# Unit 0's seven low parts move to VectorE, and pair 1's four GpSimd subtractions are issued behind pair 2's norm

## The chip, the cores and the metric

One core of a Trainium2 chip runs the kernel. The metric is the device time of one execution in microseconds (us); the time of a kernel is the median of its runs. TensorE (PE in the profile) multiplies, VectorE (DVE), ScalarE (ACT) and GpSimd (POOL) work elementwise, and SyncE's queue (SP) starts the transfers.

## What is computed

The reference is one layer of an encoder on two sequences of 512 tokens with 16 shared meta tokens in front: a convolution branch and an attention branch beside each other, then a gated feed-forward network (FFN), then a norm. The change lies where the first part ends and the FFN begins:

```python
h = h + jnp.concatenate([u, o], axis=-1) @ w_out[i]
hf = _rms(h, ffn_norm_g[i])
h = h + (jax.nn.silu(hf @ w_gate[i]) * (hf @ w_up[i])) @ w_down[i]
```

`h` is 1024 tokens by 1024, `w_gate` and `w_up` are 1024 by 2816.

## The kernel before

**High and low parts.** Every operand of a product is split in two: the high part is the float32 number cast to TensorE's fp32r format (on ACT), the low part is what the cast left over (number minus high part, one subtraction). `mm3` makes a product out of three matmuls, high by high, high by low and low by high.

**Tokens.** The 1024 tokens are eight tiles of 128, kept in `hres[0]` to `hres[7]` (in the profile `h` or `slots`). Tile t of the first sequence and tile t + 4 of the second are called pair t here. A `w_out_block` (dq, t), block (dq, t) in the text, multiplies 128 tokens by 256 columns of `w_out` and adds the result to `hres[t]` on DVE (L994). This addition is what empties PE's bank, and the text calls it the drain of the block. In the prediction, block (2,7) is columns 512 to 767 of tile 7. The banks come from `bank()`, a ring of four, which the FFN's products use as well: a block or product can begin when the drain of the fourth one before it is through.

**The norm of a pair.** `sq(t)` stores the finished `hres[t]` in DRAM, squares and sums it on ACT (L192), and on POOL adds epsilon (L193) and takes the power -1/2 (L194, the tile `rs`). `sc(t)` multiplies the tile by `rs` and the gain on DVE, in two halves (L1045, the tiles `hf` and `tt`).

**The turn of a pair.** The FFN multiplies 2 by 2 blocks in the manner of Strassen and Winograd, with seven products in place of eight, so it needs sums of the four quarters of a pair's activations. `tu(t, s)` transposes a tile on PE (L1060). `do(t, stages)` then forms the operands: stages a and A copy and cast on ACT; b takes two low parts on DVE; c, e and d form the sums on DVE (L1086, L1087, L1091, L1094) and cast them on ACT; x takes the low parts of s2 and s3, y those of s1 and s4 (all L1067). Which engine does x and y is set by the table `S_DVE`: GpSimd for pairs 0 to 2, DVE for pair 3.

**The weights.** A unit is 128 columns of `w_gate` (even units) or `w_up` (odd ones); there are 22. `comb(j)`, in the schedule `co(j)`, prepares the j-th of a unit's seven weight operands: for some j it first subtracts blocks on DVE (L1136: t1 and t2 at j = 2, t3 at 3, t4 at 5), then ACT casts the high part (L1152), then the low part is subtracted (L1154), on GpSimd unless the unit's number is in the table `U0_DVE`. `product(j)`, in the schedule `pr(j)`, is the product itself; its results are taken from the bank at L1165 to L1188.

**The order.** In this part of the kernel every instruction of PE, DVE, ACT and GpSimd is pinned, so each engine works in the order in which the program issues them. That order is a list written by hand, in which a tuple is a block and the rest are the steps named above; the seven `co` stand among the last blocks, and the list is followed by unit 0's first half-products, the turn of pair 3 (whose norm is `sc(3)` and `sc(7)`) and the other half-products. `units[1].load` loads the weights of unit 1 into `hres[2]` and `hres[6]`, once pair 2's low parts no longer need them. Each engine works through its own list, waiting where an instruction needs another engine's result.

Of the kernel before, what the change touches and what calls it, by code (L numbers as in the profile page):

```python
# [83 lines left out]
QL_DVE = False  # L84
LO_W = 1024
ORDER = "Q K S0 S1 T0 T3 M0 T1 M1 S2 T2 M2 T4 M4 M3 S3 E C"
U0_DVE = ()
S_DVE = ((), (), (), (0, 1, 2, 3))


# [11 lines left out]
def encoder_kernel(ctx: ExitStack, tc: tile.TileContext, x, meta, gains, w_in, w_kr, small, conv_w, wq, wk, wv,  # L102
# [22 lines left out]
    def pin(ins):  # L125

        return in_order(ins) if pinned[0] else ins
# [914 lines left out]
    def ffn_scale(t):  # L1042
        for e in range(2):
            h, g = (a[:, e * 512:(e + 1) * 512].rearrange("p (k n) -> p k n", k=4) for a in (hres[t], g_ffn))
            pin(nc.vector.scalar_tensor_tensor(normed_half(t, e), h, ffn_rs[t], g, ALU.mult, ALU.mult))  # L1045

    class Turn:
# [21 lines left out]
        def do(self, stages):  # L1069
            b11, b12 = self.pts[0]  # L1070
            b21, b22 = self.pts[1] if len(self.pts) > 1 else (None, None)
            t1, t2, t3, t4 = self.ts
            own = [nc.vector if i in S_DVE[self.t] else nc.gpsimd for i in range(4)]
            for stage in stages:
                if stage == "a":
                    self.high(a11, b11)
                    pin(nc.scalar.copy(t1, b11))
                    self.high(a12, b12)
                elif stage == "A":
                    pin(nc.scalar.copy(t4, b22))  # L1080
                    self.high(a22, b22)
                elif stage == "b":
                    self.low(a11, b11, nc.vector)
                    self.low(a12, b12, nc.vector)
                elif stage == "c":
                    pin(nc.vector.tensor_sub(t3, t1, b21))  # L1086
                    pin(nc.vector.tensor_sub(t1, b22, t3))  # L1087
                    self.high(s2, t1)
                    self.high(s3, t3)
                elif stage == "e":  # L1090
                    pin(nc.vector.tensor_sub(t2, b12, t1))  # L1091
                    self.high(s4, t2)
                elif stage == "d":
                    pin(nc.vector.tensor_add(t4, t4, b21))  # L1094
                    self.low(a22, b22, nc.vector)
                    self.high(s1, t4)
                elif stage == "x":
                    self.low(s2, t1, own[0])
                    self.low(s3, t3, own[1])
                elif stage == "y":  # L1100
                    self.low(s1, t4, own[2])
                    self.low(s4, t2, own[3])
# [15 lines left out]
    class Unit:  # L1118
# [19 lines left out]
        def comb(self, j):  # L1138
# [13 lines left out]
            pin(nc.scalar.copy(w[:, 0:512], src))  # L1152
            lo_eng = nc.vector if self.u in U0_DVE else nc.gpsimd
            pin(lo_eng.tensor_sub(w[:, 512:1024], src, w[:, 0:512].bitcast(F32)))  # L1154
# [96 lines left out]
    def sq(t):  # L1251
        return lambda: ffn_square(t)

    def sc(t):
        return lambda: ffn_scale(t)

    def co(j):
        return lambda: units[0].comb(j)
# [6 lines left out]
    def tu(t, s):  # L1265
        def begin():
            if not s:
                turns[t] = Turn(t)
            turns[t].turn(s)
        return begin  # L1270

    def do(t, stages):
# [5 lines left out]
         (1, 5), do(0, "ce"), (2, 5), do(0, "d"), (3, 5), sq(5), do(0, "x"),  # L1278
         (0, 2), sc(1), (1, 2), sc(5), do(0, "y"), (2, 2), (3, 2), sq(2), tu(1, 0), do(1, "a"), (0, 6), tu(1, 1), do(1, "A"),
         do(1, "b"), (1, 6), do(1, "ce"), (2, 6), do(1, "d"), (3, 6), sq(6),  # L1280
         (0, 3), sc(2), do(1, "x"), (0, 7), sc(6), co(0), do(1, "y"), (1, 3), tu(2, 0), do(2, "a"), co(1), (1, 7),
         tu(2, 1), do(2, "A"), do(2, "b"), co(2), (2, 3), co(3), do(2, "ce"), (2, 7), do(2, "d"), co(4), (3, 3), sq(3),
         co(5), (3, 7), sq(7), co(6)])

# [9 lines left out]
    def reuse(key):  # L1294
        pool = ops if key.startswith("act") else comb
        return pool.tile([P, 4, SEQ], F32R, tag=key, bufs=1, name=name("re")).rearrange("p a b -> p (a b)")
# [141 lines left out]
    y, junk = (reuse(ld_places[i]).bitcast(F32) for i in (0, 1))  # L1438
# [93 lines left out]
```

## Time and profile before

| | us |
|---|---|
| median of 3 runs | 1099.79 (1099.77 to 1099.86) |
| the profiled execution, its own time | 1100.08 |
| its span, first to last instruction | 1098.3 |
| PE busy | 1075.8 |
| DVE busy | 829.0 |
| ACT busy | 497.5 |
| POOL busy | 475.9 |

A row of the order in time gives the start in us, the time in us (of all instructions that the row merges), the engine, the line, the operation, output and inputs by the program's names, their shapes, and how many instructions the row holds; a bracket gives the idle time of the engine before it and the event that ended it. Times are counted from the span's start. An instruction's time overlaps a little with the next one's start: two drains in a row take 0.74 us, each alone 0.41. The part that the change touches lies between 440 and 482 us; the granted clock of TensorE is 1.00 there.

### The profile page before, as it was taken

To read this page: it belongs to the slowest core of one execution; us is meant where nothing else is said; L and a number is where in the kernel's file an instruction comes from. 1 tells how busy PE (TensorE), PEld (TensorE's weight loads), DVE (VectorE), ACT (ScalarE), POOL (GpSimd) and SP (SyncE) were. 2 spreads that over 40 slices of the span, in tenths; PEclk is the share of its full clock that TensorE was granted. 3 is DMA by queue.
4 is the path that set the end of the run, shared out by engine and by line. 5 is a ranking of instruction groups with operands and counts; after the bars stand their busy time and mean duration, and the time that the engine had idled before them with its cause. 6 is when DMAs were issued, how large, how long until landed. Compare 5 with 4: busy or idle time off the path is not lost.

```text
span 1098.3 us, 16027 instructions
## 1 busy us (share of the span) xinstructions
PE 1075.8 (98%) x5922; PEld 929.5 (85%) x5922; DVE 829.0 (75%) x1206; ACT 497.5 (45%) x836; POOL 475.9 (43%) x419
## 2 busy tenths in 40 slices
PE   8999999999999999899999999999999999999997
PEld 8989888888888999788888888888888888888886
DVE  5699997888887646999877876877687496656643
ACT  6554525787786534542223233322322355433331
POOL 4689735564563233775544554554555200000012
PEclk9999999999999999999999999999999999999999
DMA  7211111110100412245445426444543899865503
GB/s 295 78 39 44 44 39 61 39 55 4 40 22 35 157 58 97 77 148 186 130 160 192 169 94 207 164 140 148 201 157 103 298 329 338 293 197 182 182 22 133
DMA packets 71422, 147.08 MB, mean 134 GB/s; under 512 B 6944, under 2 KB 29728, under 8 KB 71344
## 3 DMA queue, kind: packets, MB, share of 16 engines
q1 hardware_dynamic: 71344, 146.06, 38.9%
q8 instruction: 47, 0.77, 0.3%
q14 instruction: 31, 0.25, 0.1%
HBM read 105.92 MB, written 40.11 MB: 133 GB/s over the span
## 4 chain that ended last, share of the span: by engine, by line
PE 56%; DVE 2%; issue 2%; DMA 0%; POOL 0%; ACT 0%; POOLq 0%; ACTq 0%; SPq 0%; DVEq 0%
PE pt L167 48%; PE ps L167 8%; DMA raw<-in_w_gate_dram 0%; DVE tt L1045 0%; DVE hf L1045 0%; DVE tt L1136 0%; DVE slots L994 0%; DVE act_l L1067 0%; POOL rs L194 0%; DVE h L1087 0%; POOL slots L1442 0%; DVE slots L1086 0%; DVE slots L1094 0%; DVE a12l L1067 0%; DVE h L1091 0%
## 5 line engine op out<-in xcount | busy, mean ns | idle before, releaser
L167 PE MATMUL pt<-act_h,wc 128*128 128x512 f32 (+1 forms) x552 | 175.1, 380 | 0.0
L1154 POOL TENSOR_TENSOR wc<-tt,wc 128x512 fp32r<-128x512 f32 x88 | 124.6, 1432 | 104.4 <-ACT wc L1152 60.2
L167 PEld LDWEIGHTS pt<-act_h,wc 128*128 128x128 f32 x552 | 102.5, 188 | 19.6
L193 POOL TENSOR_SCALAR ms<-ms 128x1 f32<-128x1 f32 x15 | 7.3, 485 | 242.6 <-ACT re L192 214.1
L167 PE MATMUL pt<-hn_h,wp 128*128 128x512 f32 (+2 forms) x448 | 107.0, 331 | 0.0
L167 PE MATMUL pt<-act_l,wc 128*128 128x512 f32 (+1 forms) x276 | 104.8, 380 | 0.0
L1152 ACT CAST wc<-tt 128x512 fp32r<-128x512 f32 x88 | 51.4, 617 | 116.5 <-PE pt L167 109.8
L1334 DVE TENSOR_TENSOR re<-re,re 128x1024 fp32r<-128x1024 f32 x53 | 64.1, 1223 | 45.9 <-ACT re L1333 45.8
L1333 ACT CAST re<-re 128x1024 fp32r<-128x1024 f32 x53 | 55.0, 1054 | 69.2 <-PE ps L167 20.0
L167 PE MATMUL pt<-re 128*128 128x512 f32 x360 | 84.0, 389 | 0.0
L167 PEld LDWEIGHTS pt<-hn_h,wp 128*128 128x128 f32 x448 | 75.8, 188 | 8.5
L167 PEld LDWEIGHTS pt<-re 128*128 128x128 f32 x360 | 67.6, 188 | 14.0
L152 POOL TENSOR_TENSOR wp<-raw,wp 128x1024 fp32r<-128x1024 f32 x24 | 58.5, 2439 | 40.5 <-ACT wp L149 40.5
L167 PE MATMUL pt<-hn_l,wp 128*128 128x512 f32 (+2 forms) x224 | 74.5, 332 | 0.0
L742 POOL TENSOR_SCALAR p<-p,sst 128x512 f32<-128x512 f32 x64 | 44.1, 696 | 65.3 <-DVE sst L740 57.4
L167 PE MATMUL pt<-wp,act_h 128*128 128x256 f32 x384 | 71.2, 285 | 0.0
L1154 POOL TENSOR_TENSOR wc<-raw,wc 128x512 fp32r<-128x512 f32 x33 | 45.5, 1390 | 52.1 <-ACT wc L1152 52.1
L167 PE MATMUL ps<-re 128*128 128x512 f32 x276 | 63.9, 389 | 0.0
L367 POOL TENSOR_TENSOR pacc<-pacc,prod 128x512 f32<-128x512 f32 x43 | 58.3, 1355 | 7.0 <-ACT prod L365 4.3
L167 PEld LDWEIGHTS ps<-re 128*128 128x128 f32 x276 | 51.8, 188 | 10.7
L167 PEld LDWEIGHTS pt<-act_l,wc 128*128 128x128 f32 x276 | 51.9, 188 | 9.8
L167 PEld LDWEIGHTS pt<-wp,act_h 128*128 128x128 f32 x384 | 59.9, 192 | 0.2
(296 smaller groups left out, 2937.5 us busy)
## 6 DMA issues: line engine op xcount, KB each, us to landing
raw<-in_w_gate_dram SPq DMA_DIRECT2D x22, 512.0 KB, 3.9
hf<-in_w_down_dram SPq DMA_DIRECT2D x44, 256.0 KB, 4.8
re<-in_w_down_dram SPq DMA_DIRECT2D x31, 256.0 KB, 5.3
raw<-in_w_in_dram SPq DMA_DIRECT2D x12, 512.0 KB, 3.6
slots<-in_w_up_dram SPq DMA_DIRECT2D x11, 512.0 KB, 3.5
h<-in_w_up_dram SPq DMA_DIRECT2D x11, 512.0 KB, 5.5
d_t1t<-hf SPq DMA_DIRECT2D x22, 256.0 KB, 5.4
d_t4t<-hf SPq DMA_DIRECT2D x22, 256.0 KB, 2.5
```

The source lines that it names most:

```text
L152: nc.gpsimd.tensor_sub(lo[:, a], raw[:, a], hi[:, a].bitcast(F32))
L167: pin(nc.tensor.matmul(out_ap, lhsT=w_, rhs=m_, start=first and i + j == 0, stop=last and i == n - 1 and j == 2))
L193: pin(nc.gpsimd.tensor_scalar(ms[:rows], ms[:rows], EPS, 0.0, op0=ALU.add, op1=ALU.add))
L367: nc.gpsimd.tensor_add(acc, acc, to)
L742: nc.gpsimd.tensor_scalar(pr[:, real], pr[:, real], st[:, 2, t:t + 1], 1.0, op0=ALU.mult, op1=ALU.mult)
L1152: pin(nc.scalar.copy(w[:, 0:512], src))
L1154: pin(lo_eng.tensor_sub(w[:, 512:1024], src, w[:, 0:512].bitcast(F32)))
L1333: nc.scalar.copy(w[:, :, LO], blocks[n])
L1334: nc.vector.tensor_sub(w[:, :, HI], blocks[n], w[:, :, LO].bitcast(F32))
```

## The change

The table `U0_DVE` names unit 0, so its seven low parts go from GpSimd to DVE, at the places in DVE's order where `comb` issues them. In the hand-written list, stages x and y of pair 1 are issued together behind `sc(6)`; before, x stood behind `sc(2)` and y behind `co(0)`.

```diff
-U0_DVE = ()
+U0_DVE = (0,)
...
-         (0, 3), sc(2), do(1, "x"), (0, 7), sc(6), co(0), do(1, "y"), (1, 3), tu(2, 0), do(2, "a"), co(1), (1, 7),
+         (0, 3), sc(2), (0, 7), sc(6), do(1, "xy"), co(0), (1, 3), tu(2, 0), do(2, "a"), co(1), (1, 7),
```

Both engines are shown as their instructions now stand. DVE before, from the drain of block (1,3) to t3; `pt` with a number is a bank, 5282 that of block (1,3), 5310 of (1,7), 5344 of (2,3):

```order
L994 TENSOR_TENSOR slots<-pt_5282,slots 128x256
L994 TENSOR_TENSOR slots<-pt_5310,slots 128x256
L1067 TENSOR_TENSOR act_l<-px_5296,act_h 128x4x128
L1067 TENSOR_TENSOR a12l<-px_5296,a12h 128x4x128
L1136 TENSOR_TENSOR tt_5337<-raw_4785,raw_4783 128x512
L1136 TENSOR_TENSOR tt_5339<-raw_4785,tt_5337 128x512
L994 TENSOR_TENSOR slots<-pt_5344,slots 128x256
L1136 TENSOR_TENSOR tt_5358<-raw_4785 128x512
```

The same stretch of DVE now, up to low part 3:

```order
L1154 TENSOR_TENSOR wc_5279<-raw_4783,wc_5279 128x512
L994 TENSOR_TENSOR slots<-pt_5282,slots 128x256
L1154 TENSOR_TENSOR wc_5279<-raw_4783,wc_5279 128x512
L994 TENSOR_TENSOR slots<-pt_5310,slots 128x256
L1067 TENSOR_TENSOR act_l<-px_5296,act_h 128x4x128
L1067 TENSOR_TENSOR a12l<-px_5296,a12h 128x4x128
L1136 TENSOR_TENSOR tt_5337<-raw_4785,raw_4783 128x512
L1136 TENSOR_TENSOR tt_5339<-raw_4785,tt_5337 128x512
L1154 TENSOR_TENSOR wc_5341<-tt_5339,wc_5341 128x512
L994 TENSOR_TENSOR slots<-pt_5344,slots 128x256
L1136 TENSOR_TENSOR tt_5358<-raw_4785 128x512
L1154 TENSOR_TENSOR wc_5341<-tt_5358,wc_5341 128x512
```

Low parts 0 and 1 now stand ahead of the drains of (1,3) and (1,7), low part 2 between t2, whose low part it is, and the drain of (2,3), and low part 3 directly behind t3. A little later on DVE, from pair 2's last low part to the first half of `sc(3)` (5388 is the bank of block (3,3), 5412 of (3,7), tt_5408 is t4):

```order
 L1067 TENSOR_TENSOR act_l<-px_5324,act_h 128x4x128
+L1154 TENSOR_TENSOR wc_5385<-tt_5337,wc_5385 128x512
 L994 TENSOR_TENSOR slots<-pt_5388,slots 128x256
 L1136 TENSOR_TENSOR tt_5408<-raw_4783,tt_5339 128x512
+L1154 TENSOR_TENSOR wc_5385<-tt_5408,wc_5385 128x512
 L994 TENSOR_TENSOR slots<-pt_5412,slots 128x256
+L1154 TENSOR_TENSOR wc_5432<-raw_4785,wc_5432 128x512
 L1045 SCALAR_TENSOR_TENSOR tt_5449<-slots,rs_5404,gain_4133 128x512
```

Low part 4 stands ahead of the drain of (3,3), low part 5 ahead of that of (3,7), low part 6 ahead of pair 3's norm. GpSimd's list in the same stretch, from the second subtraction of pair 1's stage x (s2l is the first) to the power for tile 7 (its addition of epsilon is the last row):

```order
 L1067 TENSOR_TENSOR act_l<-slots,act_h 128x4x128
-L1154 TENSOR_TENSOR wc_5277<-raw_4783,wc_5277 128x512
 L1067 TENSOR_TENSOR s1l<-slots,s1h 128x4x128
 L1067 TENSOR_TENSOR s4l<-h_4131,s4h 128x4x128
-L1154 TENSOR_TENSOR wc_5277<-raw_4783,wc_5277 128x512
-L1154 TENSOR_TENSOR wc_5341<-tt_5339,wc_5341 128x512
-L1154 TENSOR_TENSOR wc_5341<-tt_5358,wc_5341 128x512
-L1154 TENSOR_TENSOR wc_5385<-tt_5337,wc_5385 128x512
 L193 TENSOR_SCALAR ms_5403<-ms_5403 128x1
 L194 TENSOR_TENSOR rs_5404<-ms_5403,tiny 128x1
-L1154 TENSOR_TENSOR wc_5385<-tt_5408,wc_5385 128x512
 L193 TENSOR_SCALAR ms_5427<-ms_5427 128x1
```

The low parts are gone from GpSimd, and the other instructions stand in the order they had; the power for tile 6 stood ahead of s2l before and still does. The orders of PE, ACT and SP are the same as before.

## The prediction

> **What bounds the kernel now.** I read the busy time by stretch first, to see where TensorE (PE) loses time, then PE's waits, then the four engines' instructions in order of time around them.
>
> Busy time by stretch (start and end, length, then each engine's busy us):
>
> ```profile
> 440.00:472.00 32.00, 26.90 (x215) 25.16 (x214) 29.39 (x42) 18.26 (x35) 25.16 (x21) 1.00 0.34 109
> 472.00:1090.00 618.00, 618.00 (x2767) 513.12 (x2765) 447.85 (x551) 212.37 (x315) 216.86 (x163) 1.00 0.53 181
> ```
>
> From 472 us on PE is busy without a gap. Whatever it loses or gains in the 32 us before that moves the end one for one. In those 32 us PE idles 5.1 us and VectorE (DVE) is busy for 29.39. PE's row of time says at which instructions the idle time lies; the bracket holds the idle time before the row:
>
> ```profile
> 455.42 0.28 PE L167 MATMUL pt<-act_h,wc 128*128 128x256 f32 x1
> ...
> 458.00 0.36 PE L167 MATMUL pt<-a12h,wc 128*128 128x256 f32 x1 [0.98 <-ACT act_h L1064]
> ...
> 459.52 0.36 PE L167 MATMUL pt<-s2h,wc 128*128 128x256 f32 x1
> ...
> 464.02 1.23 PE L1060 MATMUL px<-ident,tt 128*128 128x128 f32 x8 [1.40 <-DVE tt L1045]
> ...
> 468.50 0.66 PE L1060 MATMUL px<-ident,tt 128*128 128x128 f32 x4 [0.95 <-DVE tt L1045]
> ...
> 481.95 0.40 PE L167 MATMUL pt<-act_h,wc 128*128 128x512 f32 x1
> ```
>
> 455.42, 458.00 and 459.52 are the first three products of unit 0 (first half), 464.02 and 468.50 the turns of pair 3, which wait for its norm on DVE; 481.95 is unit 1's first product. DVE in order of time:
>
> ```profile
> 443.51 1.41 DVE L1045 SCALAR_TENSOR_TENSOR hf<-h,rs,gain 128x512 f32<-128x512 f32 x2
> ...
> 445.68 3.45 DVE L1045 SCALAR_TENSOR_TENSOR hf<-slots,rs,gain 128x512 f32<-128x512 f32 x2 [0.43 <-POOL rs L194]
> 449.05 0.74 DVE L994 TENSOR_TENSOR slots<-pt,slots 128x256 f32<-128x256 f32 x2
> 449.71 0.68 DVE L1067 TENSOR_TENSOR act_l<-px,act_h 128x512 fp32r<-128x512 f32 x1
> ...
> 450.90 1.16 DVE L1136 TENSOR_TENSOR tt<-raw,raw 128x512 f32<-128x512 f32 x1
> 452.10 1.66 DVE L1136 TENSOR_TENSOR tt<-raw,tt 128x512 f32<-128x512 f32 x1
> 453.69 0.41 DVE L994 TENSOR_TENSOR slots<-pt,slots 128x256 f32<-128x256 f32 x1
> 454.02 1.45 DVE L1136 TENSOR_TENSOR tt<-raw 128x512 f32<-128x512 f32 x1
> 455.39 0.68 DVE L1086 TENSOR_TENSOR slots<-h,px 128x512 f32<-128x512 f32 x1
> ...
> 457.43 0.41 DVE L994 TENSOR_TENSOR slots<-pt,slots 128x256 f32<-128x256 f32 x1
> ...
> 458.96 0.42 DVE L994 TENSOR_TENSOR slots<-pt,slots 128x256 f32<-128x256 f32 x1
> 459.29 0.68 DVE L1136 TENSOR_TENSOR tt<-raw,tt 128x512 f32<-128x512 f32 x1
> 459.89 0.42 DVE L994 TENSOR_TENSOR slots<-pt,slots 128x256 f32<-128x256 f32 x1
> 462.12 2.42 DVE L1045 SCALAR_TENSOR_TENSOR tt<-slots,rs,gain 128x512 f32<-128x512 f32 x2 [1.82 <-POOL rs L194]
> ...
> 465.00 3.45 DVE L1045 SCALAR_TENSOR_TENSOR tt<-slots,rs,gain 128x512 f32<-128x512 f32 x2
> ...
> 474.41 0.69 DVE L1067 TENSOR_TENSOR act_l<-slots,act_h 128x512 fp32r<-128x512 f32 x1
> ```
>
> Two things are to be seen. First, the drains (L994), which empty PE's banks, stand in one line with all else on DVE. There are four banks, so product 1 needs the bank of block (2,7) (drain 457.43), product 2 that of (3,3) (458.96). PE starts 0.57 us after the one and 0.56 after the other, so I read both as bound by the drain, though the profile names ScalarE (ACT) for the first. Product 0 needs (2,3) (453.69) and product 3 needs (3,7) (459.89). PE therefore has no cushion against a later drain.
>
> Second, the same two norms cost 1.41 us at 443.51 and 3.45 at 445.68. GpSimd (POOL) stood idle at the first and subtracted during the second:
>
> ```profile
> 448.54 1.73 POOL L1154 TENSOR_TENSOR wc<-raw,wc 128x512 fp32r<-128x512 f32 x1
> 450.23 1.29 POOL L1067 TENSOR_TENSOR s1l<-slots,s1h 128x512 fp32r<-128x512 f32 x1
> 451.48 1.74 POOL L1067 TENSOR_TENSOR s4l<-h,s4h 128x512 fp32r<-128x512 f32 x1
> ...
> 466.19 1.71 POOL L1067 TENSOR_TENSOR s2l<-h,s2h 128x512 fp32r<-128x512 f32 x1
> ```
>
> A POOL subtraction takes 1.29 us alone and 1.7 beside such a DVE instruction, and DVE's t1 (450.90) ends at 452.06, 0.58 us after s1l. The two take turns whenever both of DVE's inputs lie in SBUF. The drains, which read PSUM, keep their 0.41.
>
> **The change part by part.** A low part on DVE is the form of 474.41: 0.60 us to the next instruction, alone. Seven are 4.2 us. They also free t1, t2 and t3 from POOL: 1.16, 1.66 and 1.45 come down to the 0.68 of 459.29, a relief of 0.48 + 0.98 + 0.77 = 2.2 us. That alone is +2.0 on DVE. The larger part is order. Lows 2 to 6 stand on DVE directly behind a subtraction or drain whose result ACT must first cast, so DVE waits for ACT, and the next drain waits behind it. ACT's rows give the hand-over:
>
> ```profile
> 453.80 0.62 ACT L1152 CAST wc<-tt 128x512 fp32r<-128x512 f32 x1 [2.81 <-DVE tt L1136]
> ...
> 458.48 0.62 ACT L1064 CAST s1h<-slots 128x512 fp32r<-128x512 f32 x1
> 459.00 0.62 ACT L1152 CAST wc<-tt 128x512 fp32r<-128x512 f32 x1
> 459.52 1.06 ACT L192 ACTIVATE s4l<-slots 128x1024 fp32r<-128x1024 f32 x1
> ...
> 460.57 0.60 ACT L1152 CAST wc<-tt 128x512 fp32r<-128x512 f32 x1
> ```
>
> t2 ends at 453.76, its cast starts at 453.80 and lasts 0.62. With 0.04 back to DVE (an estimate, the same as forth) that is 0.70 of waiting for each. I now follow the drains' starts. Block (1,7): POOL's s1l takes the turn of the first low part (448.54) and ends at 450.23. Low 0, ready at 449.05, waits for it and ends at 450.73. s4l then runs 1.25 to 451.98; low 1 waits for that and ends at 452.48, where the drain starts: before 449.05 + 0.33 = 449.38, so +3.1. Block (2,3): 0.33 + 1.19 for two lows + 0.71 t1 + 0.68 t2 + 0.70 hand-over + 0.60 low 2 = 4.21, before 453.69 - 449.38 = 4.31: +3.0, at 456.69. Block (2,7): 0.33 + 0.68 t3 + 0.70 + 0.60 low 3 + the 2.04 from 455.39 to 457.43 = 4.35, before 3.74: +3.6, at 461.04. Block (3,3): low 4's cast ends 459.62 - 457.43 = 2.19 after the drain, behind s1h; with 0.04 + 0.60 it is 2.83, before 1.53: +4.9, at 463.87. Block (3,7): the square of hres[3] (459.52) starts 0.45 after the drain (its 0.41 and 0.04); low 5's cast starts 1.05 later and takes 0.60, low 5 0.64: 2.74, before 0.93: +6.7, at 466.61. The first norm of pair 3: the same again with low 6: 2.74, before 462.12 - 459.89 = 2.23: +7.2, at 469.35.
>
> From there to the end of the second norm it was 468.45 - 462.12 = 6.33 us. POOL's four subtractions of pair 2 (466.19 and on) now start at about that moment. If each of four DVE norms waits for one of them, it is 2 x 3.45 + 0.33 = 7.2; if the first gets in ahead, 5.7. I take 6.5, between them, since neither end has a nearer row: +0.2. The sum is **+7.4 us**.
>
> The second edit puts no instruction elsewhere on POOL: its two subtractions already stood behind that norm's power (L194), and only the low parts between them go. s1l and s4l run 1.7 us sooner for products 4 and 6, which are far off: nothing. The loads of unit 1 stand on the SP queue behind the gain's load, which waits for the last norm, so they come some 5 to 7 us later. They are covered: the data's cast was at 477.56 and unit 1's product at 481.95, and that product moves by 7.4 as well:
>
> ```profile
> 477.56 0.62 ACT L1152 CAST wc<-h 128x512 fp32r<-128x512 f32 x1 [1.21 <-DMA h<-in_w_up_dram]
> ...
> 478.25 1.83 POOL L1154 TENSOR_TENSOR wc<-h,wc 128x512 fp32r<-128x512 f32 x1 [6.16 <-ACT wc L1152]
> ```
>
> Without that cover (low part done at 480.08, 1.87 ahead) a load that moved 7 us more than PE would cost 5.
>
> The Trainium skill, GPSIMD Engine Reference, section 4.1, says that an elementwise operation with two inputs belongs on VectorE, GpSimd being about half as fast. The rows agree (1.29 and 1.73 against 0.69); by that rule alone the time falls, which is the first rival below. Against it, the skill's Perfetto Trace Analysis, section Optimizing Scalar/DVE Operations, says that shifting work between these two might not help, because they share a port; the turns at 445.68 agree, and that is the second rival.
>
> **The rivals.** Faster: what counts is POOL. Pair 3's norm waited 1.82 us for POOL's rs, and its two halves lost 1.0 and 2.0 us to POOL's turns (2.42 and 3.45 against 1.41). If the lows fit into DVE's gaps, up to 3.5 us go: 1096.3. It decides if DVE has room, and its idle time in the stretch is 0.43 + 1.82 = 2.25 against 4.2 of lows; POOL's four subtractions of pair 2 are still there, too. Chance 0.05. No change: relief and lows trade, and PE has the remaining 2.0 hidden at most: 1099.8 to 1101.8, nearer the first only if the drains are not what PE waits for. The 0.56 of two rows speaks against it. Chance 0.05. Slower by less: the casts are ready in time, so only engine time and POOL's turns count. The waits are 0.70 each for lows 2 to 4 and 1.21 each for lows 5 and 6 (2.74 less 0.33 + 0.60 + 0.60), together 4.5; 7.4 - 4.5 = +2.9, 1102.7. It needs the casts to run ahead of DVE, and only lows 0 and 1 have theirs early. Chance 0.10. My forecast has 0.80.
>
> **How the numbers follow.** The profiled execution took 1100.08 us (span 1098.3), the median of the runs is 1099.79. The span becomes 1105.7, that execution 1107.5, the median 1099.79 + 7.4 = 1107.2. The forecast's own range: if low 0 gets ahead of s1l, term one is 1.1 smaller, and with 5.7 in the norms the sum is +5.5 (1105.3); with 7.2 and one more POOL turn of 1.25 in front of low 6 it is +9.4 (1109.2). To hold 8 in 10 the range reaches down to the milder rival: 1102.7 to 1109.2. A measurement of this kernel can tell about 0.2%, 2.2 us, from no change. Faster 0.05, same 0.05, slower 0.90.
>
> **What would show it.** Right: in the profile after, L1154 on DVE seven times; drains of (2,7) and (3,7) some 3.6 and 6.7 us later; PE's waits ahead of products 0 to 3 grown from 1 us to over 5, naming DVE; ACT idle for DVE and DVE idle for ACT by turns; t1 to t3 at 0.7; and PE gapless again after pair 3's turns. Wrong: drains at their old times, DVE without idle time for ACT's casts, or PE's wait in this stretch still near 5 us.

## The result and the profile after

The changed kernel takes 1108.28 us (median of 6 runs, 1107.55 to 1110.65) against 1099.82 of the kernel before in the same comparison (6 runs, 1099.50 to 1100.64): ratio 1.0079, 95% interval 1.0068 to 1.0090, or +8.5 us. The profiled execution after took 1107.88 us (span 1106.1), 7.8 more than the one before. The steps below are read from these two. Some executions ran for part of the time at a lower granted clock (a mean of 0.992 in the two longest runs of the changed kernel, 0.998 in the profiled one), so a difference of medians can lie up to a microsecond off that of two profiles.

Busy time by stretch, before (first fence, a stretch that is the same in both kernels) and after (second): start and end, length, then busy us and instructions of PE, PE's weight loads, DVE, ACT and POOL, and the granted clock.

```profile
440.00:480.00 40.00, 34.90 (x281) 33.16 (x280) 37.21 (x55) 22.57 (x44) 27.01 (x22) 1.00 0.37 119
```

```profile
440.00:480.00 40.00, 27.56 (x216) 25.45 (x216) 34.41 (x50) 18.44 (x35) 15.32 (x14) 1.00 0.29 95
480.00:1097.00 617.00, 617.00 (x2762) 512.66 (x2762) 447.29 (x551) 212.47 (x315) 216.18 (x162) 1.00 0.53 181
```

Nearly all of the loss lies in these 40 us: PE is busy for 27.6 us instead of 34.9, and from 480 us it has no gap, as before. DVE was given seven more instructions and yet is busy for *less* of the stretch (34.4 instead of 37.2). It isn't short of time; it waits, and the work runs out of the window to the right. PE's rows in order of time, after, to be held against the prediction's:

```profile
457.39 0.36 PE L167 MATMUL pt<-act_h,wc 128*128 128x256 f32 x1 [1.63 <-DVE slots L994]
...
461.75 0.36 PE L167 MATMUL pt<-a12h,wc 128*128 128x256 f32 x1 [2.69 <-ACT act_h L1064]
...
464.58 0.36 PE L167 MATMUL pt<-s2h,wc 128*128 128x256 f32 x1 [1.17 <-DVE slots L994]
...
476.45 0.66 PE L1060 MATMUL px<-ident,tt 128*128 128x128 f32 x4 [0.86 <-DVE tt L1045]
...
490.09 0.40 PE L167 MATMUL pt<-act_h,wc 128*128 128x512 f32 x1
```

Products 0 to 2 of unit 0, once at 455.42, 458.00 and 459.52, now start 2.0, 3.8 and 5.1 us later, and each waits; the last turn of pair 3 starts 7.95 later, and unit 1's first product 8.1 later. Product 1 names ACT, but it starts 0.56 us after a drain, just like product 2. PE's waits by what ended them (us, times, longest), from 425 to 520 us:

```profile
PE px L1060 <- DVE tt L1045: 4.3, 3, 2.5
PE pt L167 <- DVE slots L994: 3.9, 3, 1.6
PE pt L167 <- ACT act_h L1064: 2.7, 1, 2.7
```

Before, these were 2.6 us for the norm of pair 3, nothing for the drains and 1.0 for ACT. DVE in order of time, after:

```profile
449.22 1.76 DVE L1154 TENSOR_TENSOR wc<-raw,wc 128x512 fp32r<-128x512 f32 x1
450.90 0.41 DVE L994 TENSOR_TENSOR slots<-pt,slots 128x256 f32<-128x256 f32 x1
451.24 1.44 DVE L1154 TENSOR_TENSOR wc<-raw,wc 128x512 fp32r<-128x512 f32 x1
452.61 0.41 DVE L994 TENSOR_TENSOR slots<-pt,slots 128x256 f32<-128x256 f32 x1
...
454.85 0.69 DVE L1136 TENSOR_TENSOR tt<-raw,tt 128x512 f32<-128x512 f32 x1
456.22 0.69 DVE L1154 TENSOR_TENSOR wc<-tt,wc 128x512 fp32r<-128x512 f32 x1 [0.68 <-ACT wc L1152]
456.83 0.42 DVE L994 TENSOR_TENSOR slots<-pt,slots 128x256 f32<-128x256 f32 x1
457.17 0.68 DVE L1136 TENSOR_TENSOR tt<-raw 128x512 f32<-128x512 f32 x1
458.53 0.69 DVE L1154 TENSOR_TENSOR wc<-tt,wc 128x512 fp32r<-128x512 f32 x1 [0.69 <-ACT wc L1152]
...
461.19 0.41 DVE L994 TENSOR_TENSOR slots<-pt,slots 128x256 f32<-128x256 f32 x1
...
463.41 0.69 DVE L1154 TENSOR_TENSOR wc<-tt,wc 128x512 fp32r<-128x512 f32 x1 [0.61 <-ACT wc L1152]
464.02 0.42 DVE L994 TENSOR_TENSOR slots<-pt,slots 128x256 f32<-128x256 f32 x1
...
466.16 0.69 DVE L1154 TENSOR_TENSOR wc<-tt,wc 128x512 fp32r<-128x512 f32 x1 [1.13 <-ACT wc L1152]
466.77 0.42 DVE L994 TENSOR_TENSOR slots<-pt,slots 128x256 f32<-128x256 f32 x1
468.97 0.69 DVE L1154 TENSOR_TENSOR wc<-raw,wc 128x512 fp32r<-128x512 f32 x1 [1.79 <-ACT wc L1152]
469.58 3.43 DVE L1045 SCALAR_TENSOR_TENSOR tt<-slots,rs,gain 128x512 f32<-128x512 f32 x2
...
473.27 3.12 DVE L1045 SCALAR_TENSOR_TENSOR tt<-slots,rs,gain 128x512 f32<-128x512 f32 x2
```

The seven rows of L1154 are the low parts. The first two have no wait, but take 1.76 and 1.44 us in place of 0.69 (GpSimd is subtracting s1l and s4l). The other five each carry a bracket that names ACT's cast: 0.68, 0.69, 0.61, 1.13 and 1.79, together 4.9 us. In four of the five a drain or the norm follows directly, and that is what PE waits for. The last two rows are pair 3's norms, which take 3.43 and 3.12 us against 1.41 for the norm at 443.67; the cause stands in GpSimd's rows:

```profile
448.71 1.72 POOL L1067 TENSOR_TENSOR s1l<-slots,s1h 128x512 fp32r<-128x512 f32 x1
450.39 1.74 POOL L1067 TENSOR_TENSOR s4l<-h,s4h 128x512 fp32r<-128x512 f32 x1
465.70 0.23 POOL L193 TENSOR_SCALAR ms<-ms 128x1 f32<-128x1 f32 x1 [13.57 <-ACT s4l L192]
...
469.36 1.43 POOL L1067 TENSOR_TENSOR s2l<-h,s2h 128x512 fp32r<-128x512 f32 x1
...
474.11 1.73 POOL L1067 TENSOR_TENSOR s4l<-h,s4h 128x512 fp32r<-128x512 f32 x1
```

GpSimd sits idle for 13.57 us where it used to take the low parts, and then starts pair 2's four subtractions 0.22 us ahead of the norm, against which they run.

### The profile page after: what moved, and what is told of

Same layout as the page of the kernel before. It is cut to its first block, busy times and chain, and to the rows that moved or that the text cites. A ratio compares the mean times of both kernels' runs of the same rounds, so it can differ in the third digit from the quotient of the medians.

```text
span 1106.1 us, 16023 instructions
## 1 busy us (share of the span) xinstructions
PE 1076.2 (97%) x5922; PEld 930.0 (84%) x5922; DVE 833.7 (75%) x1213; ACT 497.8 (45%) x836; POOL 465.8 (42%) x412
## 4 chain that ended last, share of the span: by engine, by line
PE 56%; DVE 2%; issue 2%; ACT 1%; POOL 0%; POOLq 0%; ACTq 0%
PE pt L167 47%; PE ps L167 8%; DVE tt L1045 1%; DVE wc L1154 0%; ACT wc L1152 0%; DVE slots L994 0%; ACT s4l L192 0%; DVE tt L1136 0%; DVE hf L1045 0%; DVE h L1087 0%; DVE slots L1086 0%; POOL slots L1442 0%; DVE act_l L1067 0%; DVE a12l L1067 0%; ACT act_h L1064 0%
## 5 line engine op out<-in xcount | busy, mean ns | idle before, releaser
L1154 POOL TENSOR_TENSOR wc<-tt,wc 128x512 fp32r<-128x512 f32 x84 | 118.4, 1426 | 102.4 <-ACT wc L1152 61.0
L1154 POOL TENSOR_TENSOR wc<-raw,wc 128x512 fp32r<-128x512 f32 x30 | 40.9, 1378 | 52.6 <-ACT wc L1152 52.6
L167 PE MATMUL pt<-a12h,wc 128*128 128x512 f32 (+1 forms) x184 | 58.4, 380 | 2.7 <-ACT act_h L1064 2.7
```

The source lines that it names most:

```text
L167: pin(nc.tensor.matmul(out_ap, lhsT=w_, rhs=m_, start=first and i + j == 0, stop=last and i == n - 1 and j == 2))
```

## The experiments

Three theories of where the 8.5 us come from were held against each other. H, the forecast's: the order, in which DVE stands still for ACT's casts and the drains queue behind it. T: the turns that DVE and GpSimd take. D: DVE's time alone, the same for each of the seven low parts. Times are medians of each kernel against the kernel before on the same chip. Profiles of different kernels reach this stretch up to 1.7 us apart (`sc(2)` starts on DVE between 442.68 and 444.41, ahead of all that the edits change on DVE), and positions are compared with that taken off.

**The list's edit alone** is the changed kernel with `U0_DVE = ()`.

> Low parts stay on GpSimd, only the hand-written list is changed. All theories: 0 us against before (within 0.5), because GpSimd's second pair of subtractions only changes places with low part 0, and low part 1, for which the products wait, stays where it was. If moving those four subtractions has a cost of its own, this kernel is slower by more than 1 us.

It took 1099.73 us against 1099.83, ratio 1.0000 (0.9991 to 1.0009). The second edit costs nothing, and the 8.5 us belong to the low parts.

**Low parts 0 and 1 alone**, which have their casts early and wait for nobody:

```diff
-            lo_eng = nc.vector if self.u in U0_DVE else nc.gpsimd
+            lo_eng = nc.vector if self.u in U0_DVE and j in (0, 1) else nc.gpsimd
```

> Only low parts 0 and 1 of unit 0 go to VectorE, 2 to 6 stay on GpSimd. Theory H (the time goes into VectorE's waits for ScalarE's casts of low parts 2 to 6, with the drains behind them): +0.8 us against before, 0 to +1.5; the drain of (1,7) comes 3 us later, but it has that much room, and t1 and t2 get rid of GpSimd's turns. Rival T (the time goes into the turns in which VectorE stands behind GpSimd, first of all at low parts 0 and 1): +3 us or more, the greater part of the 8. Rival D (only VectorE's own time counts, 0.6 us for each low part less the relief): about 2/7 of the 8, +2.3 us.

It took 1100.98 us, ratio 1.0010 (1.0000 to 1.0019), +1.15 us. **The other five alone**, with `j in (2, 3, 4, 5, 6)`:

> Low parts 2 to 6 go to VectorE, 0 and 1 stay on GpSimd. H: +7.3 us against before (6 to 8.3), nearly all of it, with VectorE idle 0.7 us ahead of each of low parts 2 to 4 and more than 1 us ahead of 5 and 6. T: +2 to +4 us. D: about 5/7 of the 8, +5.7 us.

It took 1106.65 us, ratio 1.0061 (1.0044 to 1.0078), +6.8 us. From DVE's rows in order of time with low parts 0 and 1 alone, and from DVE's waits (us, times, longest) with the other five:

```profile
454.62 0.69 DVE L1136 TENSOR_TENSOR tt<-raw,tt 128x512 f32<-128x512 f32 x1
...
462.91 2.42 DVE L1045 SCALAR_TENSOR_TENSOR tt<-slots,rs,gain 128x512 f32<-128x512 f32 x2 [1.82 <-POOL rs L194]
```

```profile
DVE wc L1154 <- ACT wc L1152: 4.9, 5, 1.8
```

Low parts 0 and 1 lose their 3.1 us at drain (1,7) all the same, but the norm starts at 462.91, 0.8 later than before (462.12): t1 to t3, at 0.68 or 0.69 each, give 2.2 us back. The five bring the whole 4.9 us of waiting with them, and 6.8 of 8.5 us; by the rows, pair 3's second norm ends 6.5 us later than before, against 7.8 in the changed kernel. D, with two sevenths in the first and five in the second (2.4 and 6.0), doesn't fit the first well; T fits neither. Two of seven and five of seven is still not far from D's share, so the next run keeps all seven on DVE.

**The same five, each a few instructions later.** In the changed kernel `comb` is split, so that a low part is issued by a step of its own, `cl(j)`; the engine, the number of instructions and the data stay:

```diff
-         tu(2, 1), do(2, "A"), do(2, "b"), co(2), (2, 3), co(3), do(2, "ce"), (2, 7), do(2, "d"), co(4), (3, 3), sq(3),
-         co(5), (3, 7), sq(7), co(6)])
+         tu(2, 1), do(2, "A"), do(2, "b"), co(2), (2, 3), co(3), cl(2), do(2, "ce"), (2, 7), do(2, "d"), cl(3), co(4), (3, 3), sq(3),
+         co(5), cl(4), (3, 7), sq(7), co(6)])
...
-    run([pr(0), sc(3), pr(1), sc(7), pr(2), do(2, "xy"), units[1].load, pr(3), tu(3, 0), do(3, "a"), pr(4), do(3, "b"),
+    run([cl(5), pr(0), sc(3), pr(1), cl(6), sc(7), pr(2), do(2, "xy"), units[1].load, pr(3), tu(3, 0), do(3, "a"), pr(4), do(3, "b"),
```

> All seven low parts on VectorE as in the change, but low parts 2 to 6 stand one to three instructions later in VectorE's order, behind work that does not wait for ScalarE: 2 behind t3, 3 behind pair 2's last low part, 4 behind t4, 5 behind the drain of (3,7), 6 behind the first drain of a product. Nothing is taken away, the same instructions run on the same engines. H: most of the loss goes, +2.6 us against before remain (1.5 to 4), and VectorE's idle time for ScalarE's casts falls from 4.9 us to under 1. T and D: about as slow as the change, +7 to +9 us.

It took 1101.44 us, ratio 1.0015 (1.0005 to 1.0024), +1.6 us: with the same seven subtractions on DVE, 6.8 of the 8.5 us are gone. DVE's rows in order of time (lines are numbered some higher here: L1162 the low part, L1137 t2 to t4, L995 the drain, L1046 the norm), and its waits:

```profile
455.47 0.69 DVE L1137 TENSOR_TENSOR tt<-raw,tt 128x512 f32<-128x512 f32 x1
456.08 0.42 DVE L995 TENSOR_TENSOR slots<-pt,slots 128x256 f32<-128x256 f32 x1
456.41 0.68 DVE L1137 TENSOR_TENSOR tt<-raw 128x512 f32<-128x512 f32 x1
457.01 0.68 DVE L1162 TENSOR_TENSOR wc<-tt,wc 128x512 fp32r<-128x512 f32 x1
...
463.93 0.69 DVE L1162 TENSOR_TENSOR wc<-tt,wc 128x512 fp32r<-128x512 f32 x1 [0.19 <-ACT wc L1153]
464.54 1.41 DVE L1046 SCALAR_TENSOR_TENSOR tt<-slots,rs,gain 128x512 f32<-128x512 f32 x2
```

```profile
DVE wc L1162 <- ACT wc L1153: 0.2, 1, 0.2
```

Between t2 (455.47) and its low part (457.01) there now stand a drain and t3, 0.93 us of work, and the bracket is gone. The waits fall from 4.9 to 0.2 us. The first norm takes 1.41 again: at its end (465.95) GpSimd's subtractions had not begun (466.34). By the rows, this norm starts 5.7 us sooner than in the changed kernel, and from there to the end of the second norm it is 5.72 us in place of 6.81. So of the 6.8 us some 5.7 come of what stands ahead of the norm, and 1.1 of fewer turns with GpSimd at the norms, which the new places bring along. H is confirmed as the main account; D is out, and of T only these turns at the norms are left.

**The norms' part.** To take GpSimd's four subtractions away from pair 3's norms, the changed kernel gets one small GpSimd instruction ahead of them that reads one column of the second norm's second half, so that GpSimd waits for it. It first wrote into a new tile of 4 bytes in each partition:

```diff
+    def gate(t):
+        def begin():
+            g = const.tile([P, 1], F32, name="gate")
+            pin(nc.gpsimd.tensor_scalar(g, normed_half(t, 1)[:, 0, 0:1], EPS, 0.0, op0=ALU.add, op1=ALU.add))
+        return begin
...
-    run([pr(0), sc(3), pr(1), sc(7), pr(2), do(2, "xy"), ...
+    run([pr(0), sc(3), pr(1), sc(7), pr(2), gate(7), do(2, "xy"), ...
```

> The change, with one tiny GpSimd operation added that reads the second half of pair 3's second norm, so that GpSimd's four subtractions of pair 2 start only behind it. It prices the last term of the sum. If the two engines take turns and the norms stand behind GpSimd (6.8 us from the first norm's start to the second's end in the changed kernel): about 3.2 us in their place, so +5 us against before where the change has +8, to within 1. If those turns cost nothing on the path: +8 as the change, or more, since pair 2's low parts come later.

It took 1111.45 us, ratio 1.0105 (1.0091 to 1.0119): +11.2 us instead of +5. The same step in the kernel before, and in the kernel before with pair 1's stage x issued earlier as well (that edit is shown further down), missed by as much:

> The kernel before with only GpSimd's four subtractions of pair 2 held until pair 3's second norm is done. The theory: -1 us against before (0 to -1.5): the second norm falls from 3.45 us to about 1.4 to 2.7, behind low part 6 alone. If turns do not count: 0 or slower.

> The kernel before with both: stage x of pair 1 ahead of tile 6's square, and GpSimd's four subtractions of pair 2 held until pair 3's second norm is done. The theory: -2.8 us against before, -2 to -3.5, and so faster than both kernels. If only GpSimd's own load counts: 0 or slower, since four subtractions come later.

They took 1106.55 us (1.0056, 1.0044 to 1.0069) and 1104.75 us (1.0040, 1.0026 to 1.0054), some 7 us above what was expected of each. All three had their norms shortened as meant (1.41 and 1.41 us in the changed kernel, 2.4 and 2.4 in the other two) and lost the time elsewhere. So a control kept the tile and took the wait away: the kernel before, with the new tile written from a constant that has long been there.

```diff
+            pin(nc.gpsimd.tensor_scalar(g, ones, EPS, 0.0, op0=ALU.add, op1=ALU.add))
```

> Control: the kernel before with the added tile of one column and the tiny operation at the same place on GpSimd, but reading a constant, so that it waits for nothing. If the added tile (and with it the places of the operands in SBUF) made the last runs slow: +6 us against before, with 435 matmuls in place of 443 in each 100 us of the FFN. If the hold did it: 0.

It took 1105.71 us against 1099.79, ratio 1.0053 (1.0039 to 1.0067): without the wait the loss is there all the same, 5.9 us, so it belongs to the tile. (The second norm takes 2.43 us in the control too, 1.0 less than before, since the added instruction comes ahead of GpSimd's first subtraction. So the wait isn't what shortened it in the kernel before, and the tile's own cost may lie up to 1 us above the 5.9.) What the tile does is told in the last section. With the step's result in an unused column of a tile that was already there (`tiny[:, 39:40]` for `g`), the changed kernel gave:

> The change with GpSimd's four subtractions of pair 2 held until pair 3's second norm is done, as in the run before, but the tiny operation writes into a spare column of a tile that is there already, so that no tile is added and no address moves. If the turns in pair 3's norms are the last term of the sum: +5 us against before (within 1), 3 less than the change. If they cost nothing: +8 or more.

It took 1105.38 us, ratio 1.0047 (1.0033 to 1.0061), +5.6 us. DVE's two norms, from its rows in order of time:

```profile
470.21 1.41 DVE L1045 SCALAR_TENSOR_TENSOR tt<-slots,rs,gain 128x512 f32<-128x512 f32 x2
...
471.86 1.41 DVE L1045 SCALAR_TENSOR_TENSOR tt<-slots,rs,gain 128x512 f32<-128x512 f32 x2
```

Both now take 1.41, and from the first start to the second end it is 3.06 us in place of 6.81. Of these 3.75 us the time got 2.9 (8.46 less 5.6). What GpSimd's turns cost at the norms is real, and the kernel before had paid most of it already (6.33).

**Versions that gain.** Before the change, pair 1's x subtractions come late on GpSimd, although their inputs are ready earlier (GpSimd is idle for 6.88 us up to 444.59; with the next edit x starts at 441.41), and hold up all that follows there. In the kernel before, x is issued ahead of block (3,6):

```diff
-         do(1, "b"), (1, 6), do(1, "ce"), (2, 6), do(1, "d"), (3, 6), sq(6),
-         (0, 3), sc(2), do(1, "x"), (0, 7), sc(6), co(0), do(1, "y"), (1, 3), tu(2, 0), do(2, "a"), co(1), (1, 7),
+         do(1, "b"), (1, 6), do(1, "ce"), (2, 6), do(1, "d"), do(1, "x"), (3, 6), sq(6),
+         (0, 3), sc(2), (0, 7), sc(6), co(0), do(1, "y"), (1, 3), tu(2, 0), do(2, "a"), co(1), (1, 7),
```

> The kernel before, low parts on GpSimd, but pair 1's stage x (two subtractions) ahead of tile 6's square in the list, where GpSimd idles for 6.9 us. The theory (drains and norms of VectorE set the pace, and GpSimd's backlog slows them): -1.8 us against before, -1 to -2.5, by a GpSimd backlog that ends 2.5 us earlier. If GpSimd's backlog is without effect on the end: 0.

It took 1098.32 us against 1100.22, ratio 0.9986 (0.9977 to 0.9994), -1.9 us. DVE's rows, in order of time:

```profile
452.39 0.69 DVE L1136 TENSOR_TENSOR tt<-raw,tt 128x512 f32<-128x512 f32 x1
...
460.67 2.43 DVE L1045 SCALAR_TENSOR_TENSOR tt<-slots,rs,gain 128x512 f32<-128x512 f32 x2 [1.82 <-POOL rs L194]
```

t2 is at 0.69 us here (1.66 before) and t3 at 0.68 (1.45), since GpSimd is through with its turns by then: the relief that the change bought with seven instructions on DVE comes for nothing. The norm starts 1.45 us sooner (460.67 instead of 462.12). With the step in the spare column as well:

> The kernel before with stage x of pair 1 ahead of tile 6's square and pair 2's four subtractions held until pair 3's second norm, without an added tile. The theory of the drains and norms: -2.8 us against before (-2 to -3.5), faster than both kernels. If the hold itself was what made the last runs of this kind slow: +4 to +5, as there.

It took 1098.17 us against 1099.79, ratio 0.9983 (0.9974 to 0.9992), -1.6 us; the -2.8 expected lie at the edge of the interval, and no gain over x alone was shown. The last run puts all seven low parts on DVE, each a few instructions behind its cast (`cl(0)` behind block (2,3), `cl(1)` behind (2,7), the others as above), with x early and the step in the spare column:

> All seven low parts on VectorE but each behind work that does not wait for ScalarE (0 and 1 behind drains, too), stage x of pair 1 ahead of tile 6's square, pair 2's four subtractions held until pair 3's second norm; no tile added. The theory: -2 us against before (-1 to -3), so VectorE can take the low parts once their hand-overs are covered, but gains nothing over the same kernel with them on GpSimd (-2.8). If low parts on VectorE cost the time whatever their place: +5 or more.

It took 1098.10 us, ratio 0.9982 (0.9973 to 0.9990), -1.7 us. DVE's norms in its rows in order of time, and PE's waits (us, times, longest):

```profile
462.53 1.41 DVE L1046 SCALAR_TENSOR_TENSOR tt<-slots,rs,gain 128x512 f32<-128x512 f32 x2
...
464.78 1.41 DVE L1046 SCALAR_TENSOR_TENSOR tt<-slots,rs,gain 128x512 f32<-128x512 f32 x2
```

```profile
PE px L1061 <- DVE hf L1046: 1.8, 3, 1.0
PE pt L168 <- DVE slots L995: 0.8, 1, 0.8
```

PE no longer waits for pair 3's norm, whose rows would name `tt`, at all (4.3 us in the changed kernel, 2.6 before). The three versions with x early lie 1.6 to 1.9 us below the kernel before, with intervals wholly below 1, and can't be told from one another: the low parts can stand on DVE without loss, but no gain from their being there was seen.

## Why the prediction was right

The steps, each as the start of a row on DVE, with 0.16 us taken from the positions after (`sc(2)` starts at 443.67 instead of 443.51, ahead of the change):

| step | before | foreseen | measured |
|---|---|---|---|
| drain (1,7) | 449.38 | 452.48 | 452.45 |
| drain (2,3) | 453.69 | 456.69 | 456.67 |
| drain (2,7) | 457.43 | 461.04 | 461.03 |
| drain (3,3) | 458.96 | 463.87 | 463.86 |
| drain (3,7) | 459.89 | 466.61 | 466.61 |
| pair 3's first norm | 462.12 | 469.35 | 469.42 |
| end of the second norm | 468.45 | 475.85 | 476.23 |

**The order on DVE.** Right in each of the five drains to 0.03 us. The hand-over was put at 0.70 for lows 2 to 4 and 1.21 for lows 5 and 6, 4.5 in all; measured are 0.68, 0.69, 0.61, 1.13 and 1.79, 4.9 in all. Low 6's was under-sized by 0.6: t4 stands between the drain and low 5, but nothing stands between the next drain and low 6, so the 0.60 that was counted there as work is wait. The norm's position didn't suffer (0.07 off), since it was worked out from the chain of drain, square and cast.

**The relief.** Right: t1, t2 and t3 take 0.68, 0.69 and 0.68 us.

**The norms.** The place was right, the size was not: 6.33 us before, 6.5 taken between ends of 5.7 and 7.2, and 6.81 measured (469.58 to 476.39). GpSimd got in ahead of the first norm by 0.22 us, so the norms met nearly four turns. With the 0.07 at their start this is the 0.4 us by which the profiled execution's 7.8 exceeds the 7.4. The Trainium skill, SBUF — State Buffer, section Who interferes with whom, makes the shared port pair an exclusive lock between an instruction of VectorE with two SBUF inputs and one of GpSimd that reads SBUF; the rows agree, 1.41 us for the two halves while GpSimd was held back and 3.43 and 3.12 while it was not.

**The second edit and the loads.** Right: 1099.73 for that edit alone, and unit 1's low part is done on GpSimd at 486.17, 3.9 us ahead of the product at 490.09.

**What moved with it.** PE has no gap from 480 us on, so the end moved with the stretch. The median's +8.5 us is 0.7 above the profiled execution's 7.8, for which the granted clock named with the result is a candidate. Two other profiles show such a fall in this very stretch. With low parts 2 to 6 alone the granted clock was 0.50 from 464 to 468 us, and product 2's matmuls start 0.21 us apart there, 0.12 in the kernel before; in the changed kernel with the step in the spare column it was 0.58 from 462 to 464. So some of the time of these two kernels may be the clock's as well. The changed kernel's profile has 1.00 throughout the stretch: what the fall cost its other executions, and what sets it off, stays open.

**The signs.** PE's waits ahead of products 0 to 3 are 1.63, 2.69, 1.17 and 1.09 us, 6.6 together where over 5 was foreseen, and three of the four name DVE.

**The rivals.** Faster by freeing GpSimd (its 3.5 us aren't worked out; the three losses named with it come to 4.8): it was freed (it idles for 13.57 us), but GpSimd's `rs` is waited for no more only because DVE is later than it. Slower by less, by 2.9: its mechanism, casts that run ahead of DVE, isn't there in this order; moving the same instructions a few places made it real, at +1.6.

## What to carry to other kernels

On an engine that works in order, an instruction is costed with its wait and with what is queued behind it: here seven subtractions of 0.6 us cost 8.5 us, and 6.8 of these went when five of them were issued one to six instructions later. If a step needs another engine's answer to the instruction just ahead, put independent work between the two before judging the move. And a small control that leaves an experiment's wait out but keeps its memory shows whether the experiment itself moves the time.

## What was not expected of the hardware

**The kernel with an added tile of 4 bytes in each partition took 5.9 us longer.** The tile is written once and read by nobody, and no wait of PE in the FFN explains the loss. TensorE's instructions of the FFN after 482 us (form, count, then shortest, median and longest ns, first and last start), before and in the control:

```profile
L167 PE MATMUL pt<-act_h,wc x504: 389/389/396, 481.9 to 878.9; 128*128 128x512 f32 x168
...
L167 PE MATMUL pt<-act_l,wc x252: 389/389/398, 482.2 to 878.6; 128*128 128x512 f32 x126
...
L167 PE MATMUL pt<-s2h,wc x168: 389/389/389, 487.4 to 870.7; 128*128 128x512 f32 x168
```

```profile
L167 PE MATMUL pt<-act_h,wc x503: 392/396/397, 481.7 to 884.8; 128*128 128x512 f32 x168
...
L167 PE MATMUL pt<-act_l,wc x251: 395/396/397, 482.1 to 884.5; 128*128 128x512 f32 x126
...
L167 PE MATMUL pt<-s2h,wc x168: 389/389/389, 486.7 to 876.4; 128*128 128x512 f32 x168
```

The same 756 matmuls (two of them not recorded in the control), those with `act_h` and `act_l`, take 396 ns instead of 389; `s2h` keeps its 389. 756 times 7 ns are 5.3 us, and from the first to the last of them it is 403.1 us instead of 397.0: 6.1 us, about what the kernel lost. The same 396 ns stand in the other three kernels with the tile, and not in those that wrote into the spare column. A new tile can shift what is allocated after it; that the operands' place in SBUF is the cause is argued, not shown, and which place would matter was not tried.
